# Splitting GpSimd's subtractions and products of up to 1024 columns into instructions of 256 columns in a two-layer hybrid attention trunk

## The chip, the core and the metric

The kernel runs on one core of a Trainium2 chip. The metric is the device time of one execution in microseconds; "before" is the median of three runs. A profile is one further execution, recorded by the hardware profiler. PE is the matrix engine (PEld its weight loads), DVE the vector engine, ACT the scalar engine, POOL is GpSimd, and SP is the engine whose queue issues all of the DMAs that matter here.

## What is computed

Two layers of a transformer trunk over 512 latent and 256 context tokens of width 1024. Each layer: a modulated RMS norm, one input projection, neighbourhood attention (8 heads, window of 8 by 16 with a learned bias) and grouped-query attention (8 query heads, 2 key heads, normalised and rotated), gated merge of the two branches, output projection; then a second norm and a SwiGLU feed-forward part.

```python
h = modulate(rms_norm(x, norm1[l]), sh1, sc1)
na_q, na_k, na_v, gq, gk, gv, ga, gb = jnp.split(h @ w_in[l], IN_SPLITS, axis=-1)
bias = na_bias(na_rpb[l], in_win, dr_idx, dc_idx)
ya = merge_heads(na_latent(qa, ka, va, ka_c, va_c, bias, row_idx))
qb = apply_rope(rms_norm(heads(gq, GQA_Q_HEADS), q_gain[l]), cos, sin)
...
yb = merge_heads(ob.reshape(b, GQA_Q_HEADS, s, HEAD_DIM))
x = x + g1 * branch_merge(ya, yb, ga, gb, w_pa[l], w_pb[l], w_o[l])
h2 = modulate(rms_norm(x, norm2[l]), sh2, sc2)
x = x + g2 * swiglu(h2, w_ffn_in[l], w_ffn_out[l])
```

Everything is float32. The kernel reaches that accuracy with a reduced-precision matmul type by splitting each operand into a high and a low half: `hi` is the value rounded to the matmul type, `lo = value - hi`, and a product is three matmuls (`wh` with `h`, `wh` with `hl`, `wl` with `h`).

## The kernel before

Activations lie with the model dimension on the 128 partitions and tokens along the columns. A weight block is a tile of 128 partitions by 1024 columns (eight blocks of 128 input rows by 128 output columns), or by 512 columns for the branch projections `wp`.

Function `weight` (line 634) brings in one block: SP loads it into `wr` (four buffers), ACT copies it to the high half `wh` (three buffers, line 640), and GpSimd, or DVE where the caller says so, subtracts to get the low half `wl` (three buffers, line 642). When the subtraction has ended, the `wr` buffer is free and SP, which issues in order, can start the next load into it. Function `steps` (line 647) issues PE's matmuls block by block, three for each of the eight blocks.

Per layer there are these stages. **Mixing** (`mixing`, line 1658): attention over the heads, and projections of the input cut into small steps that fill PE while softmax runs on DVE and ACT. In layer 0 the order of PE is written out by the class `Flow`, and the framework's scheduler orders the other engines. In layer 1 the class `Plan` (line 309) orders all five: it records every operation with a cost (`cost`, line 351), due times and the tiles that it touches by region, and emits them by these (`emit`, line 419, so that the profile shows line 540 for all of them). Its cost for GpSimd stands in line 361; `begins` and `put_off` hold operations that it marks as `shared` (SBUF operations of DVE) against GpSimd's time. **Merge** (`merge`, line 1816): gates and branch projections; beside them DVE computes modulation vectors (`mod_parts`, line 718) from weights `wmodT` that pass through the same `wr` buffers. Such a weight takes two reductions on DVE in layer 0, named `junk` and `wr` in the profile. **Output projection** (`out_proj`, line 1891), whose low halves DVE makes. Then the feed-forward part, which has no GpSimd work of this kind.

GpSimd runs three kinds of wide operation, all with two SBUF inputs: the low halves `wl`; in `rope` (line 1045) the product `sh` of the shuffled query or key with the sines, 512 columns (DVE does it early in layer 1, by `self.quiet`); and per neighbourhood head the bias, negated by subtracting it from a block of zeros (lines 1764 and 1765), 768 columns for three kinds of window, of which a softmax row block reads one and the zeros (line 1446). It also computes reciprocal square roots (`hr`, `rs`), which the change leaves alone.

The names that the prediction uses, by line: `p<-p,rc` and `z<-z,rc` (1275) scale softmax rows; `m<-m,hr` (1319) scales a row minimum before the exponential; `tp` (1331, 1461) are transposes of `p` and `z` on PE; `sc` (1305) are scores; `kk` (1118) are key halves; `t<-t,mb` (1869) adds the two branches; `G<-mod` (748) are residual gates; `po` (1908) is the output projection.

Of the kernel before, what the change touches and what calls it, by code (L numbers as in the profile page):

```python
# [12 lines left out]
F32 = mybir.dt.float32  # L13
F32R = mybir.dt.float32r
AF = mybir.ActivationFunctionType
ALU = mybir.AluOpType
# [4 lines left out]
P = 128  # L21
D = 1024
KB = D // P
S = 512
# [20 lines left out]
for _n in ORDER:  # L45
    for _j in range(COLS[_n][1]):
# [17 lines left out]

BEHIND = 3.0
SLOTS = 45
ATT_P, ATT_PT = 4, 8

GA = (1, 1), (1, 1)
# [8 lines left out]
         early=0.9, reserve=8, hop=0.14, move=3.5, soon=0.5, keep=2,  # L78
# [3 lines left out]
         early=0.8, reserve=2, hop=0.2, move=3, soon=0, keep=2,  # L82
# [14 lines left out]
            g=(0.07, 0.00218, "g"), p=(0.0, 0.19, "g"))  # L97
# [211 lines left out]
class Plan:  # L309
# [41 lines left out]
    def cost(self, lane, op, aps, kw, psum):  # L351

        n = self.size(aps[0])
        scaled = hasattr(kw.get("scale"), "ap") + hasattr(kw.get("bias"), "ap")
        if lane == "p":
            wide = op != "transpose" and aps[1].dtype == F32
            return max(0.05, 4 * n * PASS / P) if wide else max(PASS, FIX + n * 0.4167e-3)
        if lane == "s":
            return n * aps[0].ap[0][1] * 4 / 0.34e6
        if lane == "g":  # L360
            return 0.31 if op == "memset" else 0.5 + n * 0.142 if n <= 16 else 0.14 + n * 0.0022
        if lane == "a":
            return 0.16 + n * 0.00088 + 0.08 * scaled + 0.1 * ("accum_out" in kw)
        if op == "tensor_reduce":
            n = self.size(aps[1])
        one = not psum and op in ("tensor_scalar", "tensor_copy", "reciprocal") and n > 16
        return 0.15 + n * (0.0006 if one else 0.00105) + 0.06 * (op == "scalar_tensor_tensor" and not psum)
# [236 lines left out]
class Trunk:  # L604
# [29 lines left out]
    def weight(self, src, cols, eng=None, pool=None):  # L634

        nc = self.nc
        raw = self.raw(src, cols)
        tile = lambda tag: (pool or self.wpool).tile([P, cols], F32R, tag="we" if pool else tag, name=self.name(tag))
        hi = tile("wh")
        nc.scalar.activation(hi, raw, AF.Copy)  # L640
        lo = tile("wl")
        (eng or nc.gpsimd).tensor_tensor(lo, raw, hi[:].bitcast(F32), op=ALU.subtract)  # L642
        if self.flow:
            self.go(("a", cols), ("v" if eng else "g", cols), at=self.flow.clock + self.plan["load"])
        return hi, lo

    def steps(self, ps, w, rhs, a, b, nk=KB, first=0):
# [397 lines left out]
    def rope(self, t, pool):  # L1045
        nc = self.nc
        sh = self.att.tile([P, T], F32, tag="rx", name=self.name("sh"))[:, :S]
        nc.vector.stream_shuffle(sh, t[:, :S], [i ^ 1 for i in range(32)])
        (nc.vector if self.flow.clock < self.quiet else nc.gpsimd).tensor_tensor(sh, sh, self.sin, op=ALU.mult)
        nc.vector.tensor_tensor(t[:, :S], t[:, :S], self.cos, op=ALU.mult)  # L1050
        nc.vector.tensor_tensor(t[:, :S], t[:, :S], sh, op=ALU.add)

# [605 lines left out]
    def mixing(self, l, h, last, at, todo, spare):  # L1658

        nc, tc, d = self.nc, self.tc, self.d  # L1660
        joint = [(0, S), (S, T)]
        spans = joint[:1] if last else joint
        n = spans[-1][1]
# [7 lines left out]
        with ExitStack() as stack:  # L1671
# [81 lines left out]
            def na(kind, head, i, done):  # L1753
# [6 lines left out]
                if head not in bias:  # L1760
                    t = bias[head] = self.wpool.tile([P, D], F32, tag="wr", name=self.name("bias"))
                    nc.sync.dma_start(t[:, 0 : 3 * 256], d["rpb"][l, head])
                    t = t[:].rearrange("p (k c) -> p k c", c=256)
                    nc.gpsimd.memset(t[:, 3], 0.0)
                    nc.gpsimd.tensor_tensor(
                        t[:, 0:3], t[:, 3:4].to_broadcast([P, 3, 256]), t[:, 0:3], op=ALU.subtract)
                if kind:
                    item = self.na_ctx(head, qs[head], keys[head], vals[head], out(ya, j), pool, done)
                else:
# [875 lines left out]
```

## Time and profile before

| | us |
|---|---|
| median of three runs | 1945.42 (1943.68 to 1946.59) |
| the profiled execution | 1943.38 |
| its span, first to last instruction | 1940.7 |
| GpSimd busy | 227.5 |
| of it low halves `wl` (67 instructions) | 152.1 |
| of it biases (16) | 30.1 |
| of it sine products (7) | 10.0 |

PE's granted clock is 0.998 on average. GpSimd works in two stretches, from 50 to 550 us (mixing and merge of layer 0) and from 1150 to 1450 us (mixing of layer 1). In a row of the groups, the parts are line, engine and operation, output and inputs, shape and count, then busy us and mean ns of one, then the idle time of the engine just before them and what ended it. In a timeline row the first two numbers are start and duration in us; an x2 at the end says that two instructions are merged, and a bracket gives the engine's idle time before it and what it waited for.

### The profile page before, as it was taken

To read this page: it belongs to the slowest core of one execution; us is meant where nothing else is said; L and a number is where in the kernel's file an instruction comes from. 1 tells how busy PE (TensorE), PEld (TensorE's weight loads), DVE (VectorE), ACT (ScalarE), POOL (GpSimd) and SP (SyncE) were. 2 spreads that over 40 slices of the span, in tenths; PEclk is the share of its full clock that TensorE was granted. 3 is DMA by queue.
4 is the path that set the end of the run, shared out by engine and by line. 5 is a ranking of instruction groups with operands and counts; after the bars stand their busy time and mean duration, and the time that the engine had idled before them with its cause. 6 is when DMAs were issued, how large, how long until landed. Compare 5 with 4: busy or idle time off the path is not lost.

```text
span 1940.7 us, 31522 instructions
## 1 busy us (share of the span) xinstructions
PE 1909.2 (98%) x12300; PEld 1764.5 (91%) x12300; DVE 1471.7 (76%) x2797; ACT 937.8 (48%) x1820; POOL 227.5 (12%) x132
## 2 busy tenths in 40 slices
PE   8999999999999999999999999999999999999998
PEld 6989999898889999999999888889988999999998
DVE  6468887769777888787868578898557587877785
ACT  4456666642226533343424345666553355544553
POOL 0432212214300000000000012132210000000000
PEclk9999999999999999999999999999999999999999
DMA  8121112235462134334443411022145532332332
GB/s 328 46 69 42 53 58 63 77 120 179 158 217 87 66 109 130 109 120 131 139 144 131 152 55 33 34 79 82 55 128 175 199 109 77 98 120 90 104 96 83
DMA packets 71670, 210.85 MB, mean 109 GB/s; under 512 B 8545, under 2 KB 10721, under 8 KB 71521
## 3 DMA queue, kind: packets, MB, share of 16 engines
q1 hardware_dynamic: 71520, 208.84, 32.9%
q8 instruction: 96, 1.57, 0.3%
q14 instruction: 54, 0.43, 0.1%
HBM read 196.75 MB, written 6.82 MB: 105 GB/s over the span
## 4 chain that ended last, share of the span: by engine, by line
PE 64%; DVE 5%; issue 1%; ACT 1%; DMA 1%; POOL 0%; SPq 0%; DVEq 0%; POOLq 0%; ACTq 0%
PE po L655 21%; PE qu L2021 14%; PE qv L2021 7%; PE pj L540 4%; PE qc L2021 3%; PE pj L655 3%; PE pf L655 3%; PE pp L655 2%; PE sc L540 2%; PE y L540 2%; PE tp L540 1%; PE pv L540 1%; ACT p L540 1%; DVE m L540 1%; DVE ptl L540 0%
## 5 line engine op out<-in xcount | busy, mean ns | idle before, releaser
L2021 PE MATMUL qu<-r,w 128*128 128x384 f32 (+1 forms) x1872 | 295.9, 310 | 0.3
L2021 PEld LDWEIGHTS qu<-r,w 128*128 128x128 f32 x1872 | 281.0, 189 | 5.0 <-DVE tt L2501 3.8
L1884 ACT ACTIVATE w<-wr 128x512 fp32r<-128x512 f32 x234 | 145.5, 625 | 107.6 <-DVE wr L2465 36.2
L655 PE MATMUL po<-ph,wh 128*128 128x512 f32 (+1 forms) x576 | 197.4, 343 | 0.0
L655 PE MATMUL po<-ph,wl 128*128 128x512 f32 (+1 forms) x576 | 196.8, 342 | 0.0
L655 PE MATMUL po<-pl,wh 128*128 128x512 f32 (+1 forms) x576 | 196.2, 341 | 0.0
L655 PE MATMUL pj<-h,wh 128*128 128x512 f32 (+1 forms) x512 | 182.1, 356 | 1.4 <-DVE ql L1256 1.1
L655 PE MATMUL pj<-h,wl 128*128 128x512 f32 (+1 forms) x512 | 176.8, 345 | 0.9 <-POOL wl L642 0.9
L655 PE MATMUL pj<-hl,wh 128*128 128x512 f32 (+1 forms) x512 | 176.6, 345 | 0.0
L1876 DVE SCALAR_TENSOR_TENSOR x<-po,G,x 128x256 f32<-128x256 f32 (+3 forms) x168 | 99.2, 596 | 100.7 <-PE po L655 99.7
L1888 DVE TENSOR_TENSOR w<-wr,w 128x512 fp32r<-128x512 f32 x234 | 159.3, 685 | 11.3 <-ACT w L1884 10.3
L640 ACT ACTIVATE wh<-wr 128x1024 fp32r<-128x1024 f32 (+1 forms) x109 | 101.3, 933 | 137.2 <-PE po L655 30.4
L2021 PE MATMUL qv<-r,w 128*128 128x384 f32 (+1 forms) x936 | 150.6, 309 | 0.3 <-ACT tt L2027 0.3
L2021 PEld LDWEIGHTS qv<-r,w 128*128 128x128 f32 x936 | 141.2, 190 | 0.5 <-ACT tt L2027 0.5
L782 POOL TENSOR_TENSOR rs<-rs,expo 128x2 f32<-128x2 f32 (+2 forms) x7 | 5.5, 784 | 1099.8 <-DVE rs L781 1099.8
L642 POOL TENSOR_TENSOR wl<-wr,wh 128x1024 fp32r<-128x1024 f32 (+1 forms) x47 | 103.5, 2205 | 229.2 <-ACT wh L640 228.9
L655 PEld LDWEIGHTS po<-ph,wl 128*128 128x128 f32 x576 | 108.2, 188 | 14.4 <-DVE wl L2192 0.4
L655 PEld LDWEIGHTS po<-pl,wh 128*128 128x128 f32 x576 | 108.5, 188 | 12.8
L655 PEld LDWEIGHTS po<-ph,wh 128*128 128x128 f32 x576 | 108.5, 188 | 12.8
L722 DVE CUSTOM_DVE_ANT_0 wr<-wr,crow 128x1024 f32<-128x1024 f32 x80 | 100.2, 1252 | 14.3 <-DMA wr<-wmodT 14.0
L655 PEld LDWEIGHTS pj<-h,wl 128*128 128x128 f32 x512 | 96.8, 189 | 13.4 <-POOL wl L642 1.3
L655 PEld LDWEIGHTS pj<-h,wh 128*128 128x128 f32 x512 | 97.0, 189 | 11.9 <-PE tp L1331 1.1
(341 smaller groups left out, 4705.7 us busy)
## 6 DMA issues: line engine op xcount, KB each, us to landing
wr<-wfi SPq DMA_DIRECT2D x88, 512.0 KB, 3.2
wr<-wmodT SPq DMA_DIRECT2D x80, 512.0 KB, 3.4
wr<-win SPq DMA_DIRECT2D x68, 512.0 KB, 3.7
wr<-wfo SPq DMA_DIRECT2D x64, 256.0 KB, 2.7
wr<-wo SPq DMA_DIRECT2D x26, 512.0 KB, 4.1
wr<-wmod SPq DMA_DIRECT2D x16, 512.0 KB, 9.9
wr<-wp SPq DMA_DIRECT2D x32, 256.0 KB, 2.9
x<-x SPq DMA_DIRECT2D x16, 384.0 KB, 7.1
```

The costliest lines, as they stand in the source:

```text
L540: ops[i]["run"](*ops[i]["args"], **ops[i]["kw"])
L640: nc.scalar.activation(hi, raw, AF.Copy)
L642: (eng or nc.gpsimd).tensor_tensor(lo, raw, hi[:].bitcast(F32), op=ALU.subtract)
L655: nc.tensor.matmul(ps[:, : b - a], u[:, c], v[k][:, a:b], start=(k == 0 and i == 0), stop=(k == nk - 1 and i == 2),)
L722: self.nc.vector.tensor_tensor_reduce(junk if s else w, w, crow[:, s], 1.0, 0.0, ALU.mult, ALU.add, self.mod[l][:, s, n : n + 1])
L782: nc.gpsimd.tensor_tensor(r[:, :nb], r[:, :nb], self.expo[:, :nb], op=ALU.pow)
L1876: self.nc.vector.scalar_tensor_tensor(x[j][:, f:u], ps[:, f - a : u - a], self.G[l][i][:, s, j : j + 1], x[j][:, f:u], op0=ALU.mult, op1=A ...
L1884: self.nc.scalar.activation(t[:, :n], src, AF.Copy)
L1888: self.nc.vector.tensor_tensor(t[:, n : 2 * n], src, t[:, :n].bitcast(F32), op=ALU.subtract)
L2021: nc.tensor.matmul(banks[bank], u[:, c], v, start=(first and k == 0 and i == 0), stop=(k == kn - 1 and i == 2), skip_group_check=True)
```

## The change

`weight` issues GpSimd's subtraction as pieces of 256 columns, four for a block of 1024 and two for one of 512; where DVE does it, it stays one instruction. `rope` does the same with GpSimd's sine product (two pieces), and the bias is negated in three. The planner's cost of a GpSimd operation and the durations that `Flow` is told are set accordingly.

```diff
+PART = 256
...
-            return 0.31 if op == "memset" else 0.5 + n * 0.142 if n <= 16 else 0.14 + n * 0.0022
+            return 0.31 if op == "memset" else 0.5 + n * 0.142 if n <= 16 else 0.2 + n * 0.00212
...
         lo = tile("wl")
-        (eng or nc.gpsimd).tensor_tensor(lo, raw, hi[:].bitcast(F32), op=ALU.subtract)
+        part = cols if eng else PART
+        for c in range(0, cols, part):
+            (eng or nc.gpsimd).tensor_tensor(
+                lo[:, c : c + part], raw[:, c : c + part], hi[:, c : c + part].bitcast(F32), op=ALU.subtract)
         if self.flow:
-            self.go(("a", cols), ("v" if eng else "g", cols), at=self.flow.clock + self.plan["load"])
+            self.go(("a", cols), *[("v" if eng else "g", part)] * (cols // part), at=self.flow.clock + self.plan["load"])
...
-        (nc.vector if self.flow.clock < self.quiet else nc.gpsimd).tensor_tensor(sh, sh, self.sin, op=ALU.mult)
+        early = self.flow.clock < self.quiet
+        part = S if early else PART
+        for c in range(0, S, part):
+            o = slice(c, c + part)
+            (nc.vector if early else nc.gpsimd).tensor_tensor(sh[:, o], sh[:, o], self.sin[:, o], op=ALU.mult)
...
-                    nc.gpsimd.tensor_tensor(
-                        t[:, 0:3], t[:, 3:4].to_broadcast([P, 3, 256]), t[:, 0:3], op=ALU.subtract)
+                    for k in range(3):
+                        nc.gpsimd.tensor_tensor(t[:, k], t[:, 3], t[:, k], op=ALU.subtract)
```

PE in the merge of layer 0, at the gate projection whose first low-half matmul starts at 467 us in the profile (`pj` is its PSUM tile, `wl_5575` the block's low half, `wl_5681` after the change). Before, with what an instruction waits for:

```order
2673 L655 MATMUL pj_5577<-h_121,wl_5575 128x512 [waits Pool_49]
2674 L655 MATMUL pj_5577<-h_123,wh_5573 128x512
2675 L655 MATMUL pj_5577<-hl_124,wh_5573 128x512
2676 L655 MATMUL pj_5577<-h_123,wl_5575 128x512
2677 L655 MATMUL pj_5577<-h_125,wh_5573 128x512
2678 L655 MATMUL pj_5577<-hl_126,wh_5573 128x512
2679 L655 MATMUL pj_5577<-h_125,wl_5575 128x512
```

And now:

```order
2673 L660 MATMUL pj_5686<-h_121,wl_5681 128x512 [waits Pool_49]
2674 L660 MATMUL pj_5686<-h_123,wh_5679 128x512
2675 L660 MATMUL pj_5686<-hl_124,wh_5679 128x512
2676 L660 MATMUL pj_5686<-h_123,wl_5681 128x512
2677 L660 MATMUL pj_5686<-h_125,wh_5679 128x512
2678 L660 MATMUL pj_5686<-hl_126,wh_5679 128x512
2679 L660 MATMUL pj_5686<-h_125,wl_5681 128x512 [waits Pool_49]
```

The sequence is the same; PE waits for GpSimd at every second low-half matmul, once for each piece, where it waited once for the whole.

GpSimd in the mixing of layer 1, at the first biases (around 1300 us). Before:

```order
103 L540 TENSOR_TENSOR wl_12159<-wr_12157,wh_12158 128x1024
104 L540 MEMSET bias_12221 128x256
105 L540 TENSOR_TENSOR bias_12221<-bias_12221 128x768
106 L540 TENSOR_TENSOR wl_12198<-wr_12196,wh_12197 128x1024
107 L540 TENSOR_TENSOR wl_12255<-wr_12253,wh_12254 128x1024
```

And now (`bias_12351` and `wl_12331` are the tiles of the rows 105 and 106 above):

```order
103 L542 TENSOR_TENSOR wl_12289<-wr_12287,wh_12288 128x256 x4
104 L542 MEMSET bias_12351 128x256
105 L542 TENSOR_TENSOR wl_12331<-wr_12329,wh_12330 128x256
106 L542 TENSOR_TENSOR bias_12351<-bias_12351 128x256 x3
107 L542 TENSOR_TENSOR wl_12331<-wr_12329,wh_12330 128x256 x3
108 L542 MEMSET bias_12388 128x256
```

One piece of the weight now stands ahead of the three pieces of the bias and three behind them.

PE in the mixing of layer 1, at the grouped-query scores that start at 1241.6 us in the profile (`sc_12026`, after the change `sc_12156`; `pj` is fill from a query projection). Before:

```order
5503 L540 MATMUL pj_12025<-h_11465,wh_11995 128x512
5504 L540 MATMUL pj_12025<-hl_11466,wh_11995 128x512
5505 L540 MATMUL pj_12025<-h_11465,wl_11996 128x512
5506 L540 MATMUL sc_12026<-kk_11858,q_11864 128x512
5507 L540 MATMUL sc_12026<-kk_11859,q_11864 128x512
```

And now:

```order
5503 L542 MATMUL pj_12155<-h_11595,wh_12125 128x512
5504 L542 MATMUL pj_12155<-hl_11596,wh_12125 128x512
5505 L542 MATMUL pj_12155<-h_11595,wl_12126 128x512
5506 L542 MATMUL pj_12155<-h_11600,wh_12125 128x512
5507 L542 MATMUL pj_12155<-hl_11601,wh_12125 128x512
5508 L542 MATMUL pj_12155<-h_11600,wl_12126 128x512
5509 L542 MATMUL sc_12156<-kk_11988,q_11994 128x512
```

Three matmuls of fill moved ahead of the scores. Such groups of three move, one way or the other, at some twenty places of this stage; PE's work is the same, and in layer 0 its sequence has not changed.

## The prediction

> **What bounds the kernel now.** I read the busy times first, then the windows by stage, then the waits of PE in the two mixing stages, then the timeline around each wait.
>
> ```profile
> PE 1909.2 (98%) x12300; PEld 1764.5 (91%) x12300; DVE 1471.7 (76%) x2797; ACT 937.8 (48%) x1820; POOL 227.5 (12%) x132
> ...
> 450.00:500.00 50.00, 49.10 (x284) 43.09 (x283) 49.46 (x74) 11.44 (x19) 19.37 (x9) 1.00 0.49 162
> 500.00:550.00 50.00, 47.56 (x272) 42.39 (x271) 36.15 (x54) 13.98 (x24) 9.38 (x5) 0.99 0.45 149
> ...
> PE po L655 <- DVE wl L642: 2.4, 1, 2.4
> ...
> PE tp L1461 <- DVE z L1275: 0.9, 1, 0.9
> PE pj L655 <- POOL wl L642: 0.9, 1, 0.9
> ...
> PE pj L540 <- ACT kg L540: 2.3, 1, 2.3
> PE sc L540 <- ACT p L540: 1.5, 3, 0.7
> PE tp L540 <- DVE z L540: 1.2, 1, 1.2
> PE sc L540 <- DVE kk L540: 0.9, 1, 0.9
> ```
>
> PE is busy 98% of 1940.7 us, so the change cannot shorten work on the path; it can only close holes in PE's stream. The windows' columns are length, PE, PEld, DVE, ACT, POOL busy, clock, DMA share, GB/s: DVE is full (49.46 of 50) in the merge of layer 0 and has room right after it. The wait rows are PE's, of 50 to 560 us (layer 0) and 1130 to 1460 us (layer 1): who waited, for whom, us in total, times, longest. Few holes, about 10 us together, and only some hang on GpSimd.
>
> How do they hang on it? By this:
>
> ```profile
> 93.25 2.37 POOL L642 TENSOR_TENSOR wl<-wr,wh 128x1024 fp32r<-128x1024 f32 x1 [14.02 <-ACT wh L640]
> ...
> 94.64 1.40 DVE L1275 TENSOR_SCALAR p<-p,rc 128x768 f32<-128x768 f32 x1
> ...
> 96.15 0.62 DVE L1275 TENSOR_SCALAR p<-p,rc 128x768 f32<-128x768 f32 x1
> ```
>
> The same DVE instruction takes 0.62 us alone and 1.40 us when it starts inside the GpSimd instruction of 93.25 to 95.62: it stands until that ends (0.98 us) and most of its own 0.62 follows. DVE instructions that read PSUM go on meanwhile. So a GpSimd instruction blocks DVE's SBUF instructions for its whole rest, and its **length** is the largest block.
>
> **The change, part by part.** First the price of a piece.
>
> ```profile
> L1049 POOL TENSOR_TENSOR sh<-sh,sin_sb x5: 1282/1297/1791, 55.4 to 182.0; 128x512 f32<-128x512 f32 x5
> ...
> L540 POOL TENSOR_TENSOR wl<-wr,wh x20: 2382/2398/2698, 1175.9 to 1418.8; 128x1024 fp32r<-128x1024 f32 x20
> ...
> L540 POOL TENSOR_TENSOR bias<-bias x8: 1837/1846/2022, 1300.6 to 1416.8; 128x768 f32<-128x768 f32 x8
> ...
> L642 POOL TENSOR_TENSOR wl<-wr,wh 128x1024 fp32r<-128x1024 f32 x31 | 77.5, 2503 | 148.9 <-ACT wh L640 148.6
> ...
> L642 POOL TENSOR_TENSOR wl<-wr,wh 128x512 fp32r<-128x512 f32 x16 | 26.1, 1628 | 80.3 <-ACT wh L640 80.3
> ```
>
> By the medians (the middle numbers, ns), 512 more columns cost 2398 - 1297 = 1101 ns, 2.15 ns a column, and 0.196 us is fixed; 768 columns give 1.847 by that, and the row says 1.846. A piece of 256 columns, which the trace does not have, is then 0.746 us; without the fixed part it would be 0.55, and the 512 row bounds it above by 1.30. I take 0.746. A weight of 1024 becomes 2.98 (+0.59), one of 512 1.49 (+0.195), a sine product 1.49 (+0.195), a bias 2.24 (+0.39). With 31 + 20, 16, 5 + 2 and 8 + 8 of them GpSimd gets 30.1 + 3.1 + 1.4 + 6.2 = 41 us more work. It has 1940 - 227 us idle, so none of that is on the path by itself: it is hidden behind PE's matmuls, which use a quarter of a weight per 1.4 us (six matmuls of 512 columns) where GpSimd makes one per 0.75 us. PE now waits per piece; before, the first low-half matmul waited for all 1024 columns. A wait that is already met costs PE nothing that the wait rows show. [...]
>
> **Layer 0, mixing.**
>
> ```profile
> 342.50 1.65 DVE L1275 TENSOR_SCALAR z<-z,rc 128x512 f32<-128x512 f32 x1
> ...
> 344.35 1.82 POOL L1765 TENSOR_TENSOR bias<-bias 128x768 f32<-128x768 f32 x1 [0.48 <-DMA bias<-rpb]
> 344.76 1.69 DVE L1275 TENSOR_SCALAR z<-z,rc 128x512 f32<-128x512 f32 x1
> ...
> 346.51 0.44 PE L1461 MATMUL tp<-ident_sb,z 128*128 128x128 f32 x2 [0.91 <-DVE z L1275]
> ```
>
> Both z scalings, 0.49 us alone, are blocked, by 1.16 and 1.20 us. In pieces each waits at most 0.75, on average half; the second ends about 1 us earlier or more, and the 0.91 us of PE go. Term: **-0.9**.
>
> **Layer 0, merge.** Here lies the doubt.
>
> ```profile
> 463.75 4.62 POOL L642 TENSOR_TENSOR wl<-wr,wh 128x1024 fp32r<-128x1024 f32 x2 [4.48 <-ACT wh L640]
> ...
> 464.81 2.40 DVE L748 TENSOR_SCALAR G<-mod 128x8 f32<-128x8 f32 x2
> ...
> 467.16 0.50 PE L655 MATMUL pj<-h,wl 128*128 128x512 f32 x1 [0.90 <-POOL wl L642]
> ...
> 519.62 4.10 POOL L642 TENSOR_TENSOR wl<-wr,wh 128x512 fp32r<-128x512 f32 x2 [6.01 <-ACT wh L640]
> 519.78 1.69 DVE L1869 TENSOR_TENSOR t<-t,mb 128x512 f32<-128x512 f32 x1
> 520.95 0.33 SPq L631 DMA_DIRECT2D wr<-wmodT  x1
> ...
> 546.12 1.22 DVE L722 CUSTOM_DVE_ANT_0 junk<-wr,crow 128x1024 f32<-128x1024 f32 x1 [4.22 <-DMA wr<-wmodT]
> ...
> 547.27 1.22 DVE L642 TENSOR_TENSOR wl<-wr,wh 128x1024 fp32r<-128x1024 f32 x1
> ...
> 548.54 0.44 PE L655 MATMUL po<-mh,wl 128*128 128x384 f32 x1 [2.44 <-DVE wl L642]
> ...
> 560.58 0.44 PE L655 MATMUL po<-mh,wl 128*128 128x384 f32 x1 [0.94 <-DVE wl L642]
> ...
> SPq L631 <- DVE mod L722: 47.9, 14, 5.2
> ```
>
> At 467.16 PE waits 0.90 us for a whole weight; its first piece would be there about 1.6 us sooner, so this hole goes. But the gain is not kept: 80 us later PE waits 2.44 us, and again 0.94, for low halves that DVE makes and that stand in its queue behind `junk`, which waits for a DMA. That DMA's start hangs on a row of buffer releases (the last row: SP waits 47.9 us, 14 times, for DVE's modulation sums), not on PE. PE that comes 0.9 us earlier waits 0.9 us longer. What counts is when this row of DVE, SP and DMA ends. At 519.62 two weights follow each other; the DMA of 520.95 leaves when the first ends. In pieces, DVE's 519.78 gets in between (0.69 us), and the release comes about 0.9 us later: two pieces 1.49 and DVE's 0.69, less the 1.30 us of now. Where DVE is full, the alternation gives back what the shorter blocks save: the nine weights of the window of 450 to 500, four of 1024 and five of 512 columns, 16.1 us of GpSimd work undisturbed, become 19.4. Against that stand gains such as at 464.81, where two DVE scalings of 8 columns cost 2.40 us, about 1.5 too much. Bounds for the end of this row: -3.4 (both waits go) and +7.5 (rival B); I take **+0.5**, near the single releases that I could follow.
>
> **Layer 1, mixing**, ordered by the planner, whose table changes too.
>
> ```profile
> 1186.02 1.84 DVE L540 TENSOR_TENSOR kk<-kg,kk 64x256 fp32r<-64x256 f32 x2
> 1186.13 1.45 POOL L540 TENSOR_TENSOR sh<-sh,sin_sb 128x512 f32<-128x512 f32 x1 [3.14 <-DVE sh L540]
> ...
> 1300.56 1.84 POOL L540 TENSOR_TENSOR bias<-bias 128x768 f32<-128x768 f32 x1 [13.41 <-DMA bias<-rpb]
> 1300.91 1.57 DVE L540 TENSOR_TENSOR m<-m,hr 128x1 f32<-128x1 f32 x2
> ...
> 1416.79 2.02 POOL L540 TENSOR_TENSOR bias<-bias 128x768 f32<-128x768 f32 x1
> ...
> 1417.24 1.85 DVE L540 TENSOR_SCALAR z<-z,rc 128x512 f32<-128x512 f32 x1
> ```
>
> Behind kk PE waits 0.9: the sine product's first half ends at 1186.88 instead of 1187.58, so 0.55 is saved. Behind the p exponentials PE waits 1.5 in three; the largest, 0.7, follows the two m products, 0.15 us each and blocked until 1302.4, now until about 1301.3: 0.7 saved. A second of the three, about 0.5, is before the scores that get three more fill matmuls ahead of them in the new order (0.7 us): saved. The tp wait of 1.2 hangs on z, 0.49 us of work in 1.85; a block of at most 0.75 saves 0.6 to 1.2, I take 0.9. Sum -2.65. The 2.3 us behind kg hang on ACT and stay. A bias that is 0.39 us later, and the moved fill, can cost something: +0.3, bounded by nothing and by the 2.65 itself. Small waits under 0.3 us that also stand behind blocked DVE work: -0.5. Term: **-2.9**.
>
> **Sum**: -0.9 + 0.5 - 2.9 = -3.3 us. The profiled execution took 1943.38 us (span 1940.7 and 2.7 around it): 1940.1 by its own time. The median of the runs is 1945.42, 2.0 above; the forecast is made for that: **1942.1 us**, 0.17% less.
>
> **Rivals.** A, more than that: in the merge shorter blocks win, both late waits (3.4) and the 0.9 at 467 go: -0.9 - 4.3 - 2.9 = -8.1, 1937.3 us. For it: the 2.40 us at 464.81 and DVE's room after 500. Against: DVE's full window, where pieces give GpSimd more turns.
> B, slower: in the full window each of the four weights of 1024 is cut by up to three DVE instructions of 1.22 us, and its input buffer is released that much later. If the last of them (3.7), the 3.3 us more of GpSimd work and the 0.5 above all pass into the row of releases, PE waits 7.5 us more at 548 and 560; with -0.9 and -2.9 that is +3.7, and with the planner's loss of 0.3 doubled +4.0, 1949.4 us. It decides from a delay of about 7.7 us. Against: the buffers are four, and single places that I followed lose about 1.
> C, DVE does not get in between queued pieces: then it stands for 2.98 where it stood for 2.40, 0.5 us more at five places, +2.5 and a little in the merge, 1948.4 us. Against: at 519.78 DVE ended at 521.47, inside the second GpSimd instruction, which was stretched (4.10 for 1.30 and 2.40). [...]
> That pieces change nothing because PE waits for the whole tile is excluded by the order: its waits stand at every second low-half matmul.
>
> **How the numbers follow.** Forecast 0.56 (spread of 2.5 us, of which 0.2 lies beyond -0.2%), A 0.2, B 0.14, C and a worse planned order within 0.2% 0.1. About 0.2%, 3.9 us, is what a measurement of this kernel tells from no change. Faster 0.40, same 0.46, slower 0.14. The range leaves the outer part of A and most of B out: 1936.5 to 1948.5.
>
> **What would show it.** GpSimd pieces of 0.70 to 0.80 us and about 265 us of GpSimd work; no z of 1.6 us and no m of 1.4 us any more; the holes at 346, 467, 1188, 1304 and 1419 gone; at 545 to 561 a PE wait behind DVE's wl that is not smaller than 2.4. If that wait is gone, A is right; if it is over 6 us, B. Wrong at the root would be pieces near 1 us, or DVE blocked over 0.75 us.

## The result and the profile after

The changed kernel took 1933.3 us (median of six runs, 1931.33 to 1936.08) where the kernel before took 1946.62 in the runs beside it (1943.68 to 1950.58): a ratio of 0.9928, 95% interval 0.9914 to 0.9941. The forecast was 1942.1, the range began at 1936.5. The profiled execution took 1933.08 us, span 1931.3.

The busy times of the page after, then the windows of the merge and the output projection of layer 0 (columns as before):

```profile
PE 1908.1 (99%) x12300; PEld 1766.6 (91%) x12300; DVE 1444.7 (75%) x2797; ACT 938.9 (49%) x1820; POOL 277.0 (14%) x340
```

```profile
450.00:500.00 50.00, 50.00 (x289) 44.18 (x289) 44.24 (x73) 11.22 (x19) 30.25 (x26) 1.00 0.52 177
500.00:550.00 50.00, 50.00 (x293) 45.62 (x292) 36.31 (x62) 17.07 (x28) 11.79 (x14) 1.00 0.54 180
```

DVE is no longer full in 450 to 500 (44.24, was 49.46) though it does nearly the same work (73 instructions, 74 before), and PE has no hole left in either window. GpSimd's busy time rose by 49.5 us, 11 of them in this one window. The groups of GpSimd after (line numbers are shifted: 642 is now 646, the planner's 540 is 542):

```profile
L646 POOL TENSOR_TENSOR wl<-wr,wh 128x256 fp32r<-128x256 f32 x156 | 133.8, 889 | 201.0 <-ACT wh L642 200.9
L542 POOL TENSOR_TENSOR wl<-wr,wh 128x256 fp32r<-128x256 f32 x80 | 60.0, 782 | 112.8 <-ACT wh L542 112.8
...
L1775 POOL TENSOR_TENSOR bias<-bias 128x256 f32<-128x256 f32 x24 | 17.3, 748 | 16.6 <-DMA bias<-rpb 16.5
```

The median piece takes 0.742 us (`wl`; 0.740 for the biases, 0.748 on average), near the 0.746 of the estimate; pieces of weights beside a busy DVE are stretched, to 0.889 us on average in layer 0 and 1.135 from 415 to 566 us. The waits of PE after, from 50 to 1460 us; of the view's rows those of layer 1:

```profile
PE pj L542 <- ACT kg L542: 2.3, 1, 2.3
...
PE sc L542 <- ACT p L542: 1.0, 2, 0.8
PE tp L542 <- DVE rc L542: 0.6, 2, 0.4
...
PE tp L542 <- DVE z L542: 0.4, 1, 0.4
...
PE sc L542 <- DVE kk L542: 0.3, 1, 0.3
```

The view has no row `po <- DVE wl` (2.4 before) and no `pj <- POOL wl` (0.9) any more, and `tp <- DVE z` is 0.4; the 2.3 behind `kg` stays. The block is as short as the pieces: of the DVE instructions that run beside a GpSimd instruction, 36 took over 0.75 us longer than their shortest like before, by up to 2.21; now none does (at most 0.74). Not all of DVE's instructions were blocked before: `z<-sc,bias`, which reads its scores from PSUM, took 0.67 to 0.69 us in all 64 cases, beside GpSimd or not, and `rc<-m`, of one SBUF column, 0.14 to 0.17 in all 160, where `z<-z,rc` took 0.47 to 1.86.

Where the time went is read best by stretches of PE between marks that every trace has: the first `tv` (mixing 0 is counted from here), the first `pp` (the merge begins), the first `po` (output projection), the first `pf` (feed-forward part), the last `tv` and the last `pj` (layer 1's mixing). The table holds the differences of their start times, in us, for all kernels of this study; a ratio is against the kernel before in the runs beside it. "Blocked" is DVE's time beyond the usual duration of the same instruction while a GpSimd low half runs, summed from 8 us ahead of the merge to 25 us into the output projection (with the median or the shortest as the usual duration it moves by up to 2 us); "late" is the mean time from the end of ACT's high half to the end of the last piece of a low half of 1024 columns there (six of them).

| kernel | median | ratio (95%) | mixing 0 | merge | out. proj. | pf to tv | mixing 1 | blocked | late |
|---|---|---|---|---|---|---|---|---|---|
| before | | | 360.9 | 118.1 | 73.5 | 568.8 | 338.2 | 21.5 | 2.9 |
| whole (before again) | 1944.26 | 0.9994 (0.9981-1.0008) | 360.8 | 118.1 | 74.1 | 568.6 | 337.8 | 20.9 | 2.9 |
| changed | 1933.30 | 0.9928 (0.9914-0.9941) | 359.3 | 116.9 | 68.3 | 570.4 | 335.3 | 9.6 | 4.3 |
| again (changed again) | 1933.81 | 0.9946 (0.9929-0.9962) | 359.3 | 117.2 | 73.3 | 568.9 | 334.7 | 14.7 | 4.3 |
| merge_only | 1941.76 | 0.9976 (0.9964-0.9989) | 360.9 | 116.9 | 67.9 | 570.5 | 338.3 | 12.4 | 4.2 |
| merge_whole | 1939.62 | 0.9970 (0.9959-0.9980) | 359.4 | 118.2 | 74.6 | 569.9 | 334.9 | 21.1 | 3.0 |
| layer1_only | 1940.76 | 0.9978 (0.9970-0.9987) | 361.0 | 118.6 | 73.5 | 570.0 | 335.2 | 21.6 | 2.9 |
| merge_reversed | 1934.46 | 0.9947 (0.9935-0.9959) | 359.4 | 118.5 | 67.9 | 570.2 | 335.0 | 10.0 | 4.4 |
| sums_cropped | 1932.18 | 0.9936 (0.9921-0.9951) | 359.3 | 116.9 | 67.9 | 570.2 | 335.0 | 17.2 | 2.6 |
| sums_longer | 1954.82 | 1.0052 (1.0037-1.0067) | 359.3 | 130.9 | 76.2 | 570.5 | 334.8 | 15.2 | 4.8 |
| merge_512 | 1936.86 | 0.9964 (0.9950-0.9978) | 359.4 | 117.1 | 72.6 | 569.9 | 335.0 | 19.6 | 3.3 |
| merge_128 | 1939.09 | 0.9969 (0.9957-0.9981) | 361.0 | 118.5 | 72.9 | 568.4 | 334.8 | 8.0 | 5.9 |
| mixing_128 | 1938.76 | 0.9975 (0.9963-0.9986) | 361.9 | 116.9 | 67.9 | 569.7 | 338.5 | 11.7 | 4.2 |
| bias_whole | 1935.95 | 0.9953 (0.9937-0.9969) | 359.3 | 116.9 | 68.0 | 568.7 | 337.7 | 12.5 | 4.3 |
| sines_whole | 1934.61 | 0.9950 (0.9932-0.9968) | 359.3 | 116.9 | 68.7 | 570.0 | 334.6 | 12.6 | 4.4 |
| quiet_14 | 1934.44 | 0.9944 (0.9930-0.9959) | 360.9 | 116.9 | 67.9 | 571.0 | 334.8 | 12.0 | 4.3 |
| sums_later | 1933.26 | 0.9928 (0.9915-0.9941) | 359.3 | 116.9 | 67.9 | 570.2 | 334.7 | 10.6 | 4.4 |
| out_gpsimd | 1934.09 | 0.9935 (0.9921-0.9949) | 359.3 | 116.9 | 68.4 | 568.7 | 335.9 | 16.0 | 4.2 |

Between the two first profiles mixing 0 gives -1.6, the merge -1.2, the output projection -5.2, mixing 1 -2.8, and `pf` to `tv`, where GpSimd has next to nothing to do, +1.5. The rest of the program is the same in all within some tenths, save for its first 60 us (62.5 to 64.7), which vary from run to run. PE's mean granted clock over the first 62 us differs too: 1.00 in the profile of before, 0.94 in that of the changed kernel (0.51 from 16.8 to 23.7 us) and in `layer1_only`, 0.97 in `merge_only`, `merge_whole` and `merge_128`. The kernel before, too, differs from one set of runs to the next: its median lies between 1944.37 and 1946.62, so a difference of one or two us between medians of different sets says little.

### The profile page after: what moved, and what is told of

It is laid out like the page before. It is cut to its first block, busy times and chain, and to the rows that moved or that the text cites. A ratio compares the mean times of both kernels' runs of the same rounds, so it can differ in the third digit from the quotient of the medians.

```text
span 1931.3 us, 31784 instructions
## 1 busy us (share of the span) xinstructions
PE 1908.1 (99%) x12300; PEld 1766.6 (91%) x12300; DVE 1444.7 (75%) x2797; ACT 938.9 (49%) x1820; POOL 277.0 (14%) x340
## 4 chain that ended last, share of the span: by engine, by line
PE 65%; DVE 5%; issue 1%; ACT 1%; DMA 1%; POOL 0%; DVEq 0%; POOLq 0%; ACTq 0%
PE po L660 21%; PE qu L2030 14%; PE qv L2030 7%; PE pj L542 6%; PE qc L2030 3%; PE pj L660 3%; PE pf L660 3%; PE pp L660 2%; PE sc L542 2%; PE y L542 2%; PE tp L542 2%; PE pv L542 1%; DMA wr<-wmodT 1%; DVE wr L727 0%; DVE z L542 0%
## 5 line engine op out<-in xcount | busy, mean ns | idle before, releaser
L646 POOL TENSOR_TENSOR wl<-wr,wh 128x256 fp32r<-128x256 f32 x156 | 133.8, 889 | 201.0 <-ACT wh L642 200.9
```

Source lines behind the costliest of these rows:

```text
L646: (eng or nc.gpsimd).tensor_tensor(lo[:, c : c + part], raw[:, c : c + part], hi[:, c : c + part].bitcast(F32), op=ALU.subtract)
```

## Experiments: where the gain lies

The diffs of this and the following sections are against the changed kernel. Three kernels split only one stage or all but one. In `merge_only` the sines, the biases and the planner's cost are those of before as well; in `layer1_only` the sines and biases of layer 0 are whole.

```diff
+        part = cols if eng else min(1024 if self.flow else 256, cols)   # merge_only
+        part = cols if eng else min(256 if self.flow else 1024, cols)   # merge_whole
+        part = cols if eng else min((256 if self.flow.plan else 1024) if self.flow else 1024, cols)   # layer1_only
```

> Only the low halves of the weights of layer 0's merge are split into pieces of 256 columns; mixing in both layers, sine products, biases and the planner's costs are as before. Theory T1 (shorter GpSimd instructions block DVE for less time, so that DVE's modulation sums, and with them the releases of the weight buffers and SP's loads, end sooner): the two PE waits of 2.44 and 0.94 us behind DVE's low halves in the output projection are gone, and the time is 4.5 to 7 us below before. Theory T2 (only the finer dependency of PE counts: the first piece is there sooner, the row of releases is not shorter): the 0.90 us at 467 goes, the two late waits stay at 3 us or more in sum, and the time is within 1.5 us of before. The prediction on record (alternation gives back what shorter blocks save) says +0.5 us.

> The changed kernel, but with the low halves of layer 0's merge in one instruction each; mixing in both layers, sine products and biases stay split. T1: the PE waits behind DVE's low halves at about 545 to 561 us return, 3 to 5 us in sum (more than before, if PE comes earlier by the 1.6 us of the mixing and the row of releases does not), and the time is 6 to 8 us above the changed kernel. T2: no more than 1.5 us above it.

> Only layer 1's mixing is split (weights, sine products, biases, with the planner's new cost); layer 0 is as before. By the prediction's term the time is 2.9 us below before; by the shift of PE's milestones between the two profiles about 1.5 to 2 us below (3.5 us gained after 1184 us, 1.5 lost before it and 0.6 lost at the end). If the loss before 1184 us comes from layer 1's own new order it is here too; if it comes from layer 0 ending earlier, it is not, and the time is some 3 us below before.

> The kernel before, once more, with its lines numbered as in the changed kernel, for a second look at its stages. Mixing of layer 0 within 0.2 us of 360.9, merge within 0.5 of 118.1, output projection within 1 of 73.5, mixing of layer 1 within 0.3 of 338.2; and the stretch from the feed-forward part of layer 0 to layer 1 (568.9 in the profile of before, 570.0 to 570.6 in nine of ten other profiles) at 570 to 570.6, if the difference is the stretch of low clock behind the pause of 2.3 us there (1166.9 to 1170.5 us in the changed kernel), which the profile of before happened not to have.

The stretches add up: the merge's pieces alone bring the merge to 116.9 and the output projection to 67.9 whatever the mixing does; without them both are as before; layer 1's pieces with the planner's new order take 3.0 us from layer 1 (4.5 by medians; no run separates the pieces from the order). By medians merge_only gave 3.5 us, less than T1's 4.5 to 7, its twelve runs spread from 1937.0 to 1947.4, and merge_whole lay 6.3 us above the changed kernel's 1933.30, as T1 had it; its holes are back too (1.1 us behind a whole low half, 3.6 us in the output projection). T2 and the prediction's +0.5 fall for the merge. In `layer1_only` the stretch from `pf` to `tv` was 570.0 with layer 1's new order, but so it was in `merge_only` (570.5) with the old one, and `again`, which has the new order and an earlier layer 0, took 568.9: neither of the two reasons in its expectation holds. `whole` missed its expectation there, with 568.6; eight of nine earlier profiles beside the one of before had 569.9 to 570.5 (the expectation says nine of ten). What differs is told below, in the section on the pause.

How does the merge gain? SP's waits from 415 to 566 us, before and after (who waits, for whom, us in total, times, longest):

```profile
SPq L631 <- DVE mod L722: 63.1, 21, 5.4
SPq L631 <- POOL wl L642: 43.3, 15, 8.2
```

```profile
SPq L633 <- POOL wl L646: 44.7, 18, 5.1
SPq L633 <- DVE mod L727: 38.9, 17, 6.3
SPq L633 <- ACT wh L642: 14.8, 6, 6.5
```

Low halves end 1.4 us later after ACT than before (4.3 for 2.9), and yet SP waits hardly longer for GpSimd. It waits 24 us less for DVE's modulation sums, and 15 us of this come back as waits for ACT's high halves. ACT in turn now waits 20.4 us for PE to be through with older high halves, where it waited 2.3 before: the row of loads runs up against PE. What such a sum costs when GpSimd is in its way, in the timelines before and after:

```profile
474.08 2.73 POOL L642 TENSOR_TENSOR wl<-wr,wh 128x1024 fp32r<-128x1024 f32 x1 [5.72 <-ACT wh L640]
...
474.48 3.41 DVE L722 CUSTOM_DVE_ANT_0 junk<-wr,crow 128x1024 f32<-128x1024 f32 x1
```

```profile
472.93 7.39 POOL L646 TENSOR_TENSOR wl<-wr,wh 128x256 fp32r<-128x256 f32 x6 [4.55 <-ACT wh L642]
...
474.70 1.76 DVE L727 CUSTOM_DVE_ANT_0 junk<-wr,crow 128x1024 f32<-128x1024 f32 x1
```

The sum takes 1.22 us alone. It stood 2.2 us behind a whole weight, and a like one stands 0.54 behind a piece.

## Experiments: the block or the first piece, DVE or GpSimd

`merge_reversed` makes the pieces of the merge from the last column to the first:

```diff
-        for c in range(0, cols, part):
+        for c in list(range(0, cols, part))[:: -1 if not eng and not self.flow else 1]:
```

> The changed kernel, but in layer 0's merge the four (or two) pieces of a low half are made from the last columns to the first, so that PE's first low-half matmul waits for the whole weight again while the blocks stay as short. T1: DVE's blocked time and the two late waits stay as in the changed kernel (gone), the hole at 467 comes back with about 1 to 2 us, and the time is 0 to 2 us above the changed kernel. T2: the whole gain of merge and output projection is lost, 6 us or more above it.

The output projection keeps all of its gain (67.9), only the merge's hole comes back (1.5 us at 464; 118.5): 1.2 us above the changed kernel. So 5.2 of the 6.4 us come with the shorter block alone, 1.2 with the first columns coming first.

Two kernels change DVE's own work instead of its waits, at 18 modulation weights of the merge:

```diff
     def mod_one(self, l, n, crow, junk):
         w = self.raw(self.d["wmodT"][l * 48 + n])
+        if l == 0 and n < 34:
+            self.nc.vector.tensor_tensor_reduce(
+                junk[:, :384], w[:, :384], crow[:, 1, :384], 1.0, 0.0, ALU.mult, ALU.add, self.mod[l][:, 1, n : n + 1])
```

This is `sums_cropped`, where it stands in place of the first of the two sums, so that the kernel leaves out the other 640 columns of that sum, with whole low halves in the merge as in `merge_whole`; in `sums_longer` it has 512 columns and stands ahead of both, and its result is overwritten.

> The kernel with the merge's low halves whole (merge_whole), but 18 of DVE's modulation reductions in the merge of layer 0 run over 384 columns where they ran over 1024 (their sums are cut short by that): about 18 x 0.65 = 11.8 us less work on DVE, as much as the split takes from DVE's blocked time there (21.5 to 9.6 us), while GpSimd's instructions keep their length. T1 (the row of releases hangs on when DVE is through, blocked or busy): the waits of the output projection (3.9 us in merge_whole) are gone, the stretch from the first po to the first pf takes 68 to 69.5 us as in the changed kernel instead of 74.5, the hole at 464 stays at about 1 us, and the time is 4.5 to 6.5 us below merge_whole. T4 (what counts is that GpSimd hands its results over in pieces): the stretch stays at 73 us or more and the time within 1.5 us of merge_whole.

> The changed kernel, but each of 18 modulation weights in the merge of layer 0 takes one more reduction of 512 columns on DVE: about 18 x 0.68 = 12.2 us more work on DVE, with GpSimd's pieces as short as in the changed kernel. T1: the waits at 545 to 561 us come back, 3 us or more in sum, the stretch from the first po to the first pf takes 72 to 76 us, and the time is 4 to 8 us above the changed kernel. T4: within 1.5 us of the changed kernel.

`sums_cropped` leaves GpSimd's weights whole, and the output projection falls to 67.9; the hole at 464, expected to stay, went too (116.9). `sums_longer` keeps the pieces and loses the output projection's gain (76.2), and 14 us in the merge besides, more than expected, where PE now waits behind ACT:

```profile
PE po L660 <- DVE wl L646: 5.2, 1, 5.2
PE pp L660 <- ACT wh L642: 3.8, 2, 2.5
PE pj L660 <- ACT wh L642: 3.2, 1, 3.2
```

Some 12 us less of DVE's time in the merge are enough for the whole gain, no matter whether they were work or waiting, and pieces without them are not: T4 falls. Why 12 us more cost 21.8 us in the two stretches, against the 6.4 that the split gained, was not followed further; low halves also end later there (4.8).

A caution on SP's waits: in `sums_cropped` they read

```profile
SPq L633 <- DVE mod L727: 69.2, 20, 8.0
SPq L633 <- POOL wl L646: 26.6, 8, 8.2
```

SP waits longer for the sums than before (63.1) and PE has no hole. So the totals by releaser do not show which link counts; the two kernels that change DVE's work do.

## Experiments: the size of a piece

`merge_512` and `merge_128` set 512 and 128 for 256 in the merge, `mixing_128` sets 128 in both mixings (weights and sines):

```diff
+        part = cols if eng else min(256 if self.flow else 128, cols)   # merge_128; 512 in merge_512
+        part = cols if eng else min(128 if self.flow else 256, cols)   # mixing_128, and 128 in rope
```

> The changed kernel, but in layer 0's merge the pieces have 512 columns (a weight of 1024 in two, one of 512 whole). T1: DVE's blocked time between 415 and 566 us lies between 9.6 (pieces of 256) and 21.5 us (whole), about 15; part of the waits of the output projection comes back, and the time is 0 to 4 us above the changed kernel. The prediction's step (alternation gives back what shorter blocks save) would have pieces of 512 no worse than 256: DVE cuts in half as often.

> The changed kernel, but in layer 0's merge the pieces have 128 columns (0.196 + 128 x 2.15 ns = 0.47 us each by the two-size estimate). T1: DVE's blocked time falls below 9.6 us, to 5 to 8; the output projection has no wait left to lose, so the time is within 1.5 us of the changed kernel. If low halves that come later were to count (eight pieces with a DVE instruction between each two: a weight of 1024 could take 7 us or more from ACT's end, where it took 4.3), PE waits for GpSimd and the time is 3 us or more above it.

> The changed kernel, but in the mixing of both layers weights and sine products are cut into pieces of 128 columns; biases and the merge stay at 256. If only the length of a block counts, the small holes of the mixing shrink further: 0 to 1.5 us below the changed kernel. If the price of more pieces counts there as it did in the merge (low halves later by 1.2 to 1.6 us with pieces of 128, and SP's loads with them), the time is 1 us or more above it; GpSimd has more room in the mixing (30 us of 100 busy) than in the merge, which speaks for the first.

Merge and output projection together take 191.6 to 192.7 us whole, 189.8 in pieces of 512, 185.2 in 256 (184.9 to 186.5 in eight other kernels with that size there, 190.6 in `again`, for which see below) and 191.4 in 128; the medians are 3.6 us (512) and 5.8 us (128) above the changed kernel's. By ratios, 0.9964 (512) and 0.9969 (128) stand against 0.9928 and 0.9946 of the changed kernel's two sets; the interval of the second set (up to 0.9962) overlaps theirs, so the order of the sizes rests on the stretches. With 512 DVE is blocked for 19.6 us, more than T1's guess of 15, and PE waits 2.5 in the output projection; the prediction's step would have had 512 no worse than 256. With 128 DVE is blocked least (8.0), but a low half of 1024 ends 5.9 us behind ACT, and where T1 had the time within 1.5 us of the changed kernel, it lies 5.8 above. SP waits longer for GpSimd:

```profile
SPq L633 <- POOL wl L646: 54.8, 18, 6.9
SPq L633 <- DVE mod L727: 37.6, 11, 7.7
```

PE itself waits 5.1 us there, behind DVE and ACT (3.0 for DVE's `wl` in the output projection), not behind GpSimd. That late low halves cause this, by way of SP's loads, fits these rows but is not shown by a run of its own. If so, what the prediction feared is real, but begins below 256 columns here. In the mixings 128 loses 2.6 us in layer 0 and 3.1 in layer 1 (where the planner's order changes with it, and where 1.6 of the 3.1 are lost at 1261 us behind a pause of 1.9, in one of the stretches at half the granted clock that the last section counts). GpSimd's room there, which spoke for a gain, did not help.

## Experiments: biases and sines

```diff
-                    for k in range(3):
-                        nc.gpsimd.tensor_tensor(t[:, k], t[:, 3], t[:, k], op=ALU.subtract)
+                    nc.gpsimd.tensor_tensor(   # bias_whole
+                        t[:, 0:3], t[:, 3:4].to_broadcast([P, 3, 256]), t[:, 0:3], op=ALU.subtract)
-        part = S if early else PART
+        part = S if early else 512   # sines_whole
```

> The changed kernel, but the biases of both layers are negated in one instruction of 768 columns again. By the prediction's steps the z scalings behind them are blocked by more than 1 us again: the hole of about 1 us at 345 returns, and the mixing of layer 0 takes about 360.5 us from its first transpose of values to the merge (before 360.9, changed 359.3); in layer 1 the waits behind m (0.7) and z (0.9) return, and the mixing takes about 336.5 to 337 us where it took 335.3 (before 338.2). The time is 2 to 3 us above the changed kernel. Rival: the weights' pieces made the gain of the mixing; then both stretches stay within 0.4 us of the changed kernel's.

> The changed kernel, but GpSimd's sine products of 512 columns are one instruction again (five in layer 0, two in layer 1). By the prediction's step 0.55 us of a hole of 1.1 us behind kk at 1187 come back (0.41 in the changed kernel), nothing else changes, and the time is 0 to 1 us above the changed kernel.

Layer 1 came out 2.4 us longer with whole biases, somewhat more than expected, and by another wait: those behind the `p` exponentials (1.0) and `z` (0.4) are as in the changed kernel, but a `p` scaling that starts 0.07 us behind a whole bias, at 1293.33, takes 2.21 us where it takes 0.62 alone, and PE waits 0.8 for it. Layer 0 did not change at all (359.3): there the rival holds. The timeline of `bias_whole` at the place of the two z scalings shows why:

```profile
343.17 0.86 DVE L1284 TENSOR_SCALAR z<-z,rc 128x512 f32<-128x512 f32 x1
...
344.64 1.20 DVE L1284 TENSOR_SCALAR z<-z,rc 128x512 f32<-128x512 f32 x1
```

```profile
339.52 5.79 POOL L646 TENSOR_TENSOR wl<-wr,wh 128x256 fp32r<-128x256 f32 x8 [9.95 <-ACT wh L642]
345.26 0.31 POOL L1773 MEMSET bias<- 128x256 f32 x1
345.65 1.91 POOL L1774 TENSOR_TENSOR bias<-bias 128x768 f32<-128x768 f32 x1
```

The eight pieces of two weights end at 345.31, after the second z has started; the bias comes when z is all but done. Before, the weights ended at 343.62, and the bias stood in the way. In the changed kernel the two z take the same 0.86 and 1.20 us (1.65 and 1.69 before). The weights' pieces shortened both, partly by making GpSimd later. With whole sines the hole behind `kk`, by the starts of the matmuls, is 0.95 again (0.41 in the changed kernel), 0.54 us more where 0.55 were expected; the rest of layer 1 came out as much shorter, and the time is the same.

## Experiments: the pause, and a wait that comes and goes

The `pf` to `tv` stretch takes 568.4 to 568.9 or 569.7 to 571.0 us, in either kernel. PE pauses 2.2 to 2.4 us behind `kg` in all of them but `quiet_14` (2.9 behind another operation). Windows of the pause, of the 3.5 us behind it and of what follows; the changed kernel first, then the kernel before (the number ahead of the DMA share is the granted clock):

```profile
1164.00:1167.00 3.00, 0.66 (x6) 0.46 (x5) 2.81 (x5) 2.45 (x7) 0.00 (x0) 1.00 0.40 87
1167.00:1170.50 3.50, 3.50 (x17) 3.50 (x18) 3.26 (x5) 0.80 (x1) 2.57 (x3) 0.52 0.80 228
1170.50:1174.00 3.50, 3.50 (x23) 3.14 (x22) 0.89 (x2) 1.33 (x2) 2.91 (x5) 0.99 0.39 151
```

```profile
545.50:548.50 3.00, 0.60 (x4) 0.28 (x2) 2.38 (x4) 0.00 (x0) 0.00 (x0) 1.00 0.00 1
548.50:552.00 3.50, 3.46 (x12) 3.20 (x12) 3.50 (x6) 0.63 (x1) 0.00 (x0) 0.56 0.74 184
...
1172.00:1175.00 3.00, 0.66 (x6) 0.45 (x5) 2.84 (x5) 2.45 (x7) 0.00 (x0) 1.00 0.40 87
1175.00:1178.50 3.50, 3.50 (x29) 3.50 (x30) 3.42 (x4) 1.34 (x2) 2.40 (x1) 1.00 0.78 220
```

Behind the pause at 1164 the clock is 0.52 for 3.5 us, and PE does 17 matmuls where it does 29 behind the same pause of the kernel before. Behind that kernel's pause at 546 it was 0.56. The last four runs turn to this and to what is left in the merge:

```diff
-         busy=2, ctx=1, vat=(1, 1), load=2.5, qt=2, rx=1, slow=(1, 1, 1), banks="tsg", lead=(2, 2, 1), quiet=28.0, spared=2, all=True),
+         busy=2, ctx=1, vat=(1, 1), load=2.5, qt=2, rx=1, slow=(1, 1, 1), banks="tsg", lead=(2, 2, 1), quiet=14.0, spared=2, all=True),   # quiet_14
-        ((0, 1, 1, 1, 1, 1, 1, 1), (1, 2, 2, 2, 2, 2, 1, 0), (1, 1, 1, 1, 1, 1, 1, 0)),   # MODS, layer 0
+        ((0, 1, 1, 1, 1, 1, 1, 1), (1, 2, 2, 2, 2, 2, 1, 0), (0, 1, 1, 1, 1, 1, 1, 1)),   # sums_later
-                    ws[j] = self.weight(self.d["wo"][l, j], D, self.nc.vector)
+                    ws[j] = self.weight(self.d["wo"][l, j], D, None if l == 0 and half == 0 and j < 4 else self.nc.vector)   # out_gpsimd
```

> The changed kernel, but at the start of layer 1's mixing one more weight's low half and one sine product go to GpSimd (in pieces of 256 columns), where DVE made them in one instruction each; DVE's 1.21 us low half at 1164.24 stood ahead of what ACT's kg waits for, and PE waits 2.34 us for kg at 1164.29. Theory P (a pause of 2.3 us or more costs its own length and mostly some 1.5 us more, by a stretch of about 3.5 us at half the clock behind it; shorter pauses cost only their length): the pause falls to 1.1 us or less, the clock stays full behind it, and the stretch from the feed-forward part of layer 0 to layer 1 takes 567 to 568 us where it took 570.4; the time is 1 to 3 us below the changed kernel. Rival: the pause moves to another place in the start of layer 1, or the clock drops without a long pause; then no gain.

> The changed kernel once more: 1931.3 to 1936.1 us as in its first six runs; behind its pause at 1164 us the clock is low in most profiles (then 570 to 570.6 us from the feed-forward part of layer 0 to layer 1), or stays full (then 568.5 to 568.9).

> The changed kernel, but the seven modulation sums that stand beside the first seven blocks of layer 0's output projection stand beside blocks two to eight: DVE's low half of the first block has no reduction ahead of it, and SP loads it one modulation weight sooner. T1: the wait at 543 to 546 us is gone in every profile, the stretch from the first po to the first pf takes 68 to 69 us, and the slower part of the changed kernel's runs (1936 to 1939) goes: median 1931 to 1933.5, highest run under 1937. Rival: the reductions come back as a wait at the end of the first half of the output projection (the second norm needs the sums): 1 us or more above the changed kernel.

> The changed kernel, but GpSimd makes the low halves of the first four blocks of layer 0's output projection, in pieces of 256 columns, where DVE made them (4 x 1.22 us) in its queue behind the reductions. T1: DVE has 4.9 us less to do, but is blocked again by up to 16 pieces; the waits at 543 to 560 us are gone or under 1 us, the time within 2 us of the changed kernel. Rival: GpSimd's low halves (4.3 us from ACT's end to the last piece in the merge, where DVE takes 1.2) are late for PE themselves: waits for GpSimd there, 2 us or more above the changed kernel.

`quiet_14` failed as a test: the pause grew (by 0.55 us between the starts of the matmuls around it), so it says nothing on shorter pauses, and theory P's bound of 2.3 us is not shown; the stretch rose to 571.0. What stands is the count in the last section, not an experiment of its own.

`again` is the surprise: its runs reach beyond both ends of what was expected, and the changed kernel has the pause of the output projection in its second profile:

```profile
PE po L660 <- DVE wl L646: 3.2, 2, 2.8
```

The two profiles part at small things. The same sum, with the GpSimd pieces beside it, in the first profile of the changed kernel and in `again`:

```profile
444.41 1.22 DVE L727 CUSTOM_DVE_ANT_0 junk<-wr,crow 128x1024 f32<-128x1024 f32 x1
...
444.56 3.13 POOL L646 TENSOR_TENSOR wl<-wr,wh 128x256 fp32r<-128x256 f32 x2 [1.17 <-ACT wh L642]
```

```profile
444.78 2.42 POOL L646 TENSOR_TENSOR wl<-wr,wh 128x256 fp32r<-128x256 f32 x2 [0.99 <-ACT wh L642]
...
444.81 1.80 DVE L727 CUSTOM_DVE_ANT_0 junk<-wr,crow 128x1024 f32<-128x1024 f32 x1
```

Where DVE starts 0.15 us ahead of the piece it goes through in 1.22 us, where it starts 0.03 behind it takes 1.80. Such turns summed to 14.7 us of blocked time instead of 9.6, SP's load that left at 541.02 us left 5.5 us later, and the wait was there. This chain is read from two profiles, not shown by a run; `out_gpsimd`, with 16.0 us blocked, has no such wait. The twelve runs of the changed kernel range from 1929.94 to 1938.98. `sums_later`, which takes one sum from the head of DVE's queue in the output projection, takes 67.9 us there, as the shortest do, and runs from 1930.57 to 1934.31, median 1933.26. It is not shown to be faster than the changed kernel, though its highest run lies under the changed kernel's (1936.08 and 1938.98 in its two sets); one profile and six runs are not enough to say that the wait never comes. `out_gpsimd` came out at 1934.09, with no wait of more than 0.4 us there: pieces on GpSimd do as well as DVE.

## Why the prediction was wrong

**The step that failed** is the merge term, +0.5: "Where DVE is full, the alternation gives back what the shorter blocks save". Merge and output projection gave -6.4, and these 6.9 us are most of the 8.8 by which the time fell below the forecast. Both halves of that balance were real, but the saving was never added up: DVE is blocked for 12 us less, of which the prediction priced one place, 464.81, at 1.5 us (there it is 2.1: two scalings of 0.16 alone took 2.40). The delay was about rightly sized: a low half of 1024 ends 1.4 us later, where 0.9 was reckoned at one release. And the two lie on different links of the row of releases. SP's row hung on when DVE was through: `sums_cropped` reaches 116.9 and 67.9 with whole low halves, and `sums_longer` loses them with pieces. GpSimd's releases had slack: low halves that end 2.6 us behind ACT (`sums_cropped`) and 4.3 us (the changed kernel) give the same merge within 0.1 us and the same output projection within 0.4. A delay on the link with slack was set against a gain on the one without. Where that slack ends lies between 4.3 and 5.9 us, if the reading of `merge_128` is right.

**Rival A** is what happened, and its size was too small. It gave the merge and the output projection -4.3; they gave -6.4 (-1.2 and -5.2). The excess is mostly the low clock behind the pause at 546: from 548.5 to 552.0 PE did 12 matmuls at 0.56 of the clock, for which at the pace of the next window (23 in 4.0 us) 2.1 us are enough. So a pause of 2.4 us was priced at 2.4 and cost about 3.8. **Rival B** (releases delayed until PE waits) fits pieces of 128, not of 256. **Rival C** did not occur, DVE gets in between queued pieces: the `x6` row at 472.93 took 7.39 us where six pieces of 0.746 take 4.48, and DVE's sum of 474.70 began and ended in it.

**Layer 0, mixing**: -0.9 forecast, -1.6 measured; the place was right (both z, the hole at 346), the agent wrong: the weights' pieces did it, not the bias's.

**Layer 1, mixing**: -2.9 forecast, -2.8 and -3.5 in the two profiles of the changed kernel. The wait behind kk fell from 0.9 to 0.3 (0.55 forecast; the two ends that the prediction names, 1186.88 and 1187.58, are 0.70 apart), behind z from 1.2 to 0.4 (0.9), behind the p exponentials from 1.5 to 1.0 (1.2 forecast, too much), and a new wait of 0.6 behind rc came up. These rows give -1.3; by the starts of the matmuls, where smaller holes count in full, all holes over 0.15 us fell from 6.6 to 4.1. One saving did not come: the three matmuls of fill that moved ahead of the scores at 1241.6 were taken from the fill ahead of the scores at 1255.1, whose wait grew from 0.27 to 0.97 us. So the sum came out nearly right, in part by luck. The 2.3 behind kg stayed, as said.

**The price of a piece**, 0.746 us: 0.742 measured, by the median. GpSimd's work came to 277.0 us where about 265 was said (268.5 by the 227.5 of before and the 41 reckoned), since pieces that alternate with DVE are stretched (1.135 us on average from 415 to 566 us).

**The sum**: by these stretches -10.8, of which the first profiles show -9.4, because the changed one had the low clock behind the pause at 1164 (0.52) and the one before had not (1.00). The medians differ by 13.3 us in the first set of runs and by 10.9 in that of `again`; in the first the kernel before had its highest median (1946.62), and what the 13.3 hold beyond the stretches stays open.

## What to carry to other kernels

When an edit makes one engine's work shorter in the way and another's later, put each on the link of the chain that it feeds before setting one against the other, and add up each over the whole stage instead of following single places. The waits of the queue in the middle (here SP's, by releaser) do not say which link has slack; a run that shortens or lengthens one engine's own work does. Two engines that block each other can have a best piece between the longest block and the lateness of the whole (of the four sizes here, 256 columns). Where the row is tight, the outcome of the turns differs from run to run, so a single profile of such a kernel can lack the very wait that another has (here 68.3 and 73.3 us for the output projection in two profiles of one kernel). A pause of the matrix engine cost more than its length here in most cases: behind 20 of the 28 of 2.5 to 5.5 us, 1.5 us or more on top.

## What the runs showed of the hardware

Of the 28 pauses of PE from 60 us on, in the eighteen profiles, with 2.5 to 5.5 us between the matmuls' starts, 20 were followed by 3.4 us (two by 6.8) at half the granted clock (the 0.52 and 0.56 over 3.5 us above), which lost 1.5 to 2.0 us (2.5 and 2.6); behind the same pause of 2.62 us at the start of layer 1 it comes in some runs and not in others, with the same instructions around it. Of five pauses of 1.6 to 2.1 us one was followed by such a stretch. It also came at 170 us in `merge_128` and `quiet_14` (a clock of 0.69 and 0.58 from 170 to 174 us, 1.00 in the changed kernel), behind a hole of 0.7 us by the starts of the matmuls and twelve matmuls of 128x2, which the changed kernel has too: that is most of the 1.6 us more of these two in the column of mixing 0.
